# The first FFN half-step computed from an x that is loaded with features on partitions and left unscaled, with the inverse roots applied behind the products

## The chip, the core and the metric

The kernel runs on one core of one Trainium2 chip. The time is device microseconds of one execution; several runs of a kernel agree within about 0.2%. The profile is taken from one execution by the hardware profiler. TensorE is called PE (its weight loads PEld), VectorE DVE, ScalarE ACT, GpSimd POOL; SP only issues DMAs. SBUF has 128 partitions; matmul results go to banks of PSUM, 128 x 512 words of float32 each.

## What is computed

One layer of a decoder block for 1024 tokens of 1024 features in float32. The change lies in the first half-step and touches nothing behind it:

```python
def rms_norm(x, g):
    xf = x.astype(jnp.float32)
    y = xf * lax.rsqrt(jnp.mean(xf * xf, axis=-1, keepdims=True) + RMS_EPS)
    return (y * g.astype(jnp.float32)).astype(x.dtype)

def swiglu(x, w1, w3, w2):
    return (jax.nn.silu(x @ w1) * (x @ w3)) @ w2

h = h + 0.5 * swiglu(rms_norm(h, ffn1_norm[l]), ffn1_w1[l], ffn1_w3[l], ffn1_w2[l])
# then the mixers, h = h + merged @ w_out[l], the second half-step and the last norm
```

`w1` and `w3` are 1024 x 2816, `w2` is 2816 x 1024. The root in `rms_norm` is one number for each token, the gain `g` one for each feature.

## The kernel before, in words

**Seven products.** Each large matrix product is made from 2 x 2 blocks with seven products in place of eight (class `Sevens`, L306). For `x @ w1` the blocks of x are the halves of the tokens and of the features, with features on partitions: b11 and b21 are the low and high features of tokens 0 to 511, b12 and b22 those of tokens 512 to 1023. The seven right operands are b11, b21, b22 and the sums t1 = b12 - b11, t2 = b22 - t1, t3 = b22 - b12 and t4 = t2 - b21. Every operand is held as a high part in a rounded type and a low part, the remainder; ACT makes the high part and DVE or POOL the low one, and a product takes three of the four combinations: twelve matmuls of 128 x 512 (`product`, L325).

**Pairs and quads.** The 22 column blocks of each factor are taken two at a time: 11 pairs (class `Pair`, L565), each with a quad A of `w1` and a quad B of `w3` (class `Quad`, L336). A quad's weight blocks come as two rows, `raw`, of 512 KB. `operand(m)` forms the weight operand m and splits it into four rotating places `wc`; `run(m)` issues the product. Products 1 and 2 of a quad, with b11 and b21, add up in one bank; 3 and 5 in another. `a_out` and `b_out` take a bank's contents: for m = 1 ACT copies it before m = 2 may add to it, for m = 2 of quad A a silu follows. From the opening on there are four banks of each of the two kinds (`mm`, `acc`).

**The opening** (`begin_up1`, L981, an order written out by hand, as are all parts under `manual_schedule`: each engine runs its instructions in the order in which they are written). Rows of x, 128 tokens each, are loaded, squared on ACT, their roots taken on POOL (`inverse`, L277), and multiplied by root and gain on DVE. Then PE transposes them, four 128 x 128 pieces at a time, into a bank (`Rows`, L402; `turned` in `Entry.run`, L483), from which ACT takes the high part and DVE the low part and the sums. While the first rows are on their way, four products of pairs 4 and 5 are made from x loaded with features on partitions (`led_run`); they are scaled later by the roots spread over columns (`means`), stored in DRAM and fetched in pairs 4 and 5. The first two products of pairs 0 to 2 run between the transposes.

**Behind it.** `up` (L692) runs the other five products of pairs 0 to 2 by hand, operands two products ahead of their use, then pairs 3 to 9, whose order the framework sets, then pair 10 by hand. `Down` (L778) multiplies by `w2`, with tokens on partitions, and `add` (L871) adds half of each result to the rows of x.

Loads of x and of weights go through SP's queue in order of writing; the gains and the rows of x for `add` through ACT's.

Of the kernel before, what the change touches and what calls it, by code (L numbers as in the profile page):

```python
# [16 lines left out]
P = 128  # L17
# [120 lines left out]
def tile_block(  # L138
# [145 lines left out]
    def scaled_part(t, c, gain):  # L284
        ve.scalar_tensor_tensor(h[t][:, c], h[t][:, c], inv[t][:, 1:2], gain[:, c], op0=OP.mult, op1=OP.mult)

# [19 lines left out]
    class Sevens:  # L306


        def __init__(self, name, X, fw, fs=None):
            self.name, self.X, self.fw, self.fs = name, X, fw, fs or fw  # L310
            self.n_lo = 0
            self.terms = (0, 1, 2)
            self.led = {}
# [251 lines left out]
    class Pair:  # L565
# [3 lines left out]
        def __init__(self, sv, j, sums, early=False, spare=False):  # L569


            self.sv, self.j, self.sums = sv, j, sums
            self.place_of = [h_tile if spare else tmp, h_tile if early else tmp]
            self.u2 = (lambda n: h_tile(f"u2_{n}")[:, :HALF]) if spare else (lambda n: sv.half_tile("u", n))
            self.y = []
            self.A, self.B = Quad(sv, f"{j}a"), Quad(sv, f"{j}b")
            self.u = {}
            self.led = sv.led.get(j)
            self.order = ORDER if self.led is None else (2, *(m for m in ORDER if m not in (1, 2)))
# [5 lines left out]

        def fetch_a(self):
            if self.led is not None:
                nc.sync.dma_start(self.place(0, slice(HALF, S)), self.led[0])

        def fetch_b(self):  # L590
            if self.led is not None:
                self.u[2] = self.u2(f"{self.j}2")
                nc.sync.dma_start(self.u[2], self.led[1])
# [7 lines left out]
        def a_out(self, m, p):  # L601
# [7 lines left out]
            elif m == 2:  # L609
                c = self.place(0, lows)  # L610
                if self.led is not None:
                    ve.tensor_tensor(c, p, u2, op=OP.add)
                    p = c
# [3 lines left out]
            elif m == 5:  # L617
                c22 = self.place(1, highs)
                ve.tensor_tensor(c22, p, self.place(1, lows), op=OP.add)
                ac.activation(c22, c22, AF.Silu)  # L620
            elif m == 4:
                u3 = self.place(1, lows)
                ve.scalar_tensor_tensor(u3, p, -1.0, u3, op0=OP.mult, op1=OP.add)
                ac.activation(u3, u3, AF.Silu)
            else:
                ve.tensor_tensor(u2, p, u2, op=OP.add)
                ac.activation(u2, u2, AF.Silu)

        def b_out(self, m, p):
# [7 lines left out]
            elif m == 2:  # L637
                c = self.place(0, lows)
                if self.led is not None:
                    u[3] = self.sv.half_tile("u", f"{j}3")  # L640
                    ve.tensor_tensor(u[3], p, u[2], op=OP.add)
                    p = u[3]
                ve.tensor_tensor(c, p, c, op=OP.mult)
            elif m == 7:
                if 3 not in u:
                    u[3] = self.sv.half_tile("u", f"{j}3")
# [45 lines left out]
    def up(sv, sums, between, name, room, begun):  # L692
# [31 lines left out]
        for j in range(len(begun), NPAIR - 1):  # L724
            q, then = then or Pair(sv, j, sums), None
            for m in q.order[:3]:
                q.a(m)
            q.fetch_b()
            for m in q.order[3:]:
                q.a(m)  # L730
            if j == NPAIR - 2:
                between()
            if j + 1 in sv.led:
                then = Pair(sv, j + 1, sums)
                then.fetch_a()
            for m in q.order[:-2]:
                q.b(m)
# [4 lines left out]
            for m in q.order[-2:]:  # L742
                q.b(m)
# [34 lines left out]
    class Down:  # L778
# [3 lines left out]
        def __init__(self, name, sums, half_tile, pair):  # L782
# [7 lines left out]
            self.right, self.apart = {}, set()  # L790
            downs.append(self)
# [139 lines left out]
    for t in range(NT):  # L931
        h.append(h_tile(f"x{t}"))

    def load_rows(*ts):
        for t in ts:
            nc.sync.dma_start(h[t], x[t * P:(t + 1) * P, :])

    gain_row = keep.tile([P, D], F32, tag="gain", bufs=1, name="gain_ffn1")
    led_x, led_in = [], []
    for n in range(2):  # L940
        led_x.append(row(f"led_x{n}").rearrange("p (k c) -> p k c", k=2))
        led_in.append(row(f"led_w{n}").rearrange("p (k c) -> p k c", k=2))
    square = X["t1"][0][:, 0:2, :].rearrange("p k c -> p (k c)")
    square2 = tmp("square2")

    LED = (4, 5)
    led_dram = [dram.tile([P, HALF], F32, name=f"led{q}") for q in range(4)]

    def load_all():
        def features(kk):  # L950
            nc.sync.dma_start(led_x[kk], x_t[0, kk])

        def weight(q):
            nc.sync.dma_start(led_in[q // 2][:, q % 2], (w1a, w3a)[q % 2][2 * LED[q // 2]][:, LOWS])

        features(0)
        weight(0)
        weight(1)
        features(1)
        load_rows(0)  # L960
        weight(2)
        load_rows(1)
        weight(3)
        load_rows(2, 3)
        raws.depth = 2
        raws.load()
        load_rows(4)
        raws.depth = 3
        raws.load()
        load_rows(5)  # L970
        raws.depth = 4
        raws.load()
        load_rows(6, 7)
        raws.depth = 6
        raws.load()
# [5 lines left out]
    def begin_up1():  # L981


        load_all()
        idle = bank("mm", "idle")

        def keep_on(n):

            for _ in range(n):
                pe.matmul(idle[:, :P], ones, ones, start=True, stop=True)  # L990

        def spread(p, columns):
            for k, c in enumerate(columns):
                pe.transpose(p[:, k * P:(k + 1) * P], c.to_broadcast([P, P]), ident)
            return p

        def gains(b):
            return spread(bank("acc", f"gain{b}"), [gain1[:, k:k + 1] for k in range(4 * b, 4 * b + 4)])

        def gain_copy(b):  # L1000
            ac.activation(gain_row[:, (LOWS, HIGHS)[b]], g[b], AF.Copy)

        r = {}

        def rows(t, what, c, tag="acc", eng=ac):
            r[t] = Rows(X, what, h[t][:, c], t, tag, eng=eng)

        def first_scaled(t):
            ve.scalar_tensor_tensor(h[t][:, LOWS], h[t][:, LOWS], inv[t][:, 1:2], g[0], op0=OP.mult, op1=OP.mult)

        xhi, xlo = X["t4"]
        kept = [sv1.half_tile("s", f"led{q}") for q in range(4)]
        means = sv1.half_tile("u", "means")
        led_w, led_p = {}, {}

        def led_high(k, eng=ac):
            if eng is ac:
                ac.activation(xhi[:, k], led_x[k // 2][:, k % 2], AF.Copy, scale=gain1[:, k:k + 1])
            else:
                ve.tensor_scalar(xhi[:, k], led_x[k // 2][:, k % 2], gain1[:, k:k + 1], None, op0=OP.mult)  # L1020

        def led_low(k):
            ve.scalar_tensor_tensor(xlo[:, k], led_x[k // 2][:, k % 2], gain1[:, k:k + 1], xhi[:, k].bitcast(F32),
                                    op0=OP.mult, op1=OP.subtract)

        def led_split(q, c):
            if q not in led_w:
                led_w[q] = fp.tile([P, 2, HALF], F32R, tag="wc", bufs=4, name=f"wc_led{q}")
            w, src = led_w[q], led_in[q // 2][:, q % 2]
            ac.activation(w[:, 0, c], src[:, c], AF.Copy)  # L1030

        def led_rest(q, c):
            w, src = led_w[q], led_in[q // 2][:, q % 2]
            gp.tensor_tensor(w[:, 1, c], src[:, c], w[:, 0, c].bitcast(F32), op=OP.subtract)

        FRONT, BACK, WHOLE = slice(0, 2 * P), slice(2 * P, HALF), slice(0, HALF)
        count = {}

        def led_run(q, ks, terms):
            w = led_w[q]  # L1040
            if q not in led_p:
                led_p[q] = bank("mm", f"u_led{q}")
                count[q] = 0
            for i in terms:
                for k in ks:
                    r = slice(k * P, (k + 1) * P)
                    a, b = three((w[:, 0, r], w[:, 1, r]), (xhi[:, k, :], xlo[:, k, :]))[i]
                    pe.matmul(led_p[q], a, b, start=count[q] == 0, stop=count[q] == 11)
                    count[q] += 1

        def led_scaled(q):
            ve.tensor_tensor(kept[q], kept[q] if q < 2 else led_p[q], means, op=OP.mult)
            nc.sync.dma_start(led_dram[q], kept[q])
            sv1.led.setdefault(LED[q // 2], [None, None])[q % 2] = led_dram[q]

        keep_on(13)
        led_high(0)
        led_high(1, ve)
        led_split(0, FRONT)
        led_split(0, BACK)  # L1060
        led_rest(0, FRONT)
        led_low(0)
        led_low(1)
        led_rest(0, BACK)
        led_split(1, FRONT)
        led_rest(1, FRONT)
        led_split(1, BACK)
        led_rest(1, BACK)
        led_run(0, (0, 1), (0, 1, 2))
        g = {}  # L1070
        for b in (1, 0):
            g[b] = gains(b)
        led_run(1, (0, 1), (0, 1, 2))
        led_high(2)
        led_high(3, ve)
        led_low(2)
        led_low(3)
# [1433 lines left out]
```

## Time and profile before

| what | us |
|---|---|
| median of 3 runs | 1885.16 (1884.06 to 1885.36) |
| the profiled execution | 1884.1 |
| its span | 1882.3 |
| mean granted clock of PE | 0.999 of full speed |
| first matmul of a product | 6.38 from the span's start |
| first matmul of `Down` of the first half-step | 434.3 |

A page of a profile gives each engine's busy time and a strip of 40 slices of the span, one digit for tenths of busy time. Other views list groups of equal instructions, the instructions in order of time (start, duration, name, and in brackets the engine's idle time and what ended it) and busy time in chosen stretches. In names like `u_f10a` the letters behind f1 are pair and quad: pair 0, quad A. Matmuls overlap: one lasts 0.39 us and the next begins 0.23 us after it began.

### The profile page before, as it was taken

The page shows a single profiled execution, that of the slowest core. Times are in us where ns is not written, and L with a number is a line of the kernel's source. Part 1 is how long each engine was busy: PE and PEld are TensorE (multiplying, and loading weights), DVE is VectorE, ACT ScalarE, POOL GpSimd, SP SyncE. Part 2 cuts the span into 40 slices and gives each one's busy share as a digit, 9 for nine tenths or more (in the row PEclk, how much of TensorE's full clock was granted, in tenths as well). Part 3 has the DMA queues.
Part 4 walks back from the last instruction along what each step waited for, and adds up shares of the span by engine and source line. Part 5 has one row for each costly group of instructions (what it writes and reads, how often), then busy time and mean ns, then how long its engine had stood idle before and what let it go on. Part 6 is the DMA issues. An engine that isn't in the chain of part 4 may idle for free.

```text
span 1882.3 us, 24614 instructions
## 1 busy us (share of the span) xinstructions
PE 1872.2 (99%) x8758; PEld 1554.8 (83%) x8758; DVE 1349.0 (72%) x1981; ACT 773.4 (41%) x1395; POOL 727.7 (39%) x543
## 2 busy tenths in 40 slices
PE   9999999999999999999999999999999999999998
PEld 8888888888888888888888888888888888888886
DVE  7877666558786776658885897787765566577867
ACT  7433333334344543334445772363333333334344
POOL 4533333331223364444554457545333333312221
PEclk9999999999999999999999999999999999999999
DMA  6154323336565526765578878634332233354654
GB/s 248 56 201 163 128 100 116 115 118 222 177 224 196 182 91 221 243 219 188 209 254 315 313 227 294 262 147 172 125 139 85 89 107 111 136 200 156 225 197 146
DMA packets 146035, 334.98 MB, mean 178 GB/s; under 512 B 17784, under 2 KB 39288, under 8 KB 144376
## 3 DMA queue, kind: packets, MB, share of 16 engines
q1 hardware_dynamic: 142168, 322.55, 49.7%
q10 hardware_dynamic: 3744, 10.85, 1.6%
q8 instruction: 69, 1.13, 0.2%
q14 instruction: 54, 0.44, 0.1%
HBM read 232.76 MB, written 100.60 MB: 177 GB/s over the span
## 4 chain that ended last, share of the span: by engine, by line
PE 54%; DVE 3%; ACT 2%; issue 1%; DMA 1%; POOL 1%; ACTq 0%; SPq 0%; DVEq 0%; POOLq 0%
PE u_mixm L332 15%; PE d_f L869 8%; PE wo L2191 4%; PE yp L1933 1%; PE u_f20a L332 1%; PE u_f21b L332 1%; PE u_f20b L332 1%; PE u_f21a L332 1%; PE u_f210b L332 1%; PE u_f210a L332 1%; PE u_f29b L332 1%; PE u_f29a L332 1%; PE u_f28b L332 1%; PE u_f28a L332 1%; PE u_f27b L332 1%
## 5 line engine op out<-in xcount | busy, mean ns | idle before, releaser
L869 PE MATMUL d_f<-bhi_f,ahi_f 128*128 128x512 f32 x616 | 240.2, 390 | 0.0
L869 PE MATMUL d_f<-bhi_f,alo_f 128*128 128x512 f32 x616 | 239.7, 389 | 0.0
L869 PE MATMUL d_f<-blo_f,ahi_f 128*128 128x512 f32 x616 | 239.6, 389 | 0.0
L826 POOL TENSOR_TENSOR alo_f<-g_f,ahi_f 128x512 fp32r<-128x512 f32 x60 | 86.0, 1450 | 273.6 <-ACT ahi_f L822 273.6
L332 PE MATMUL u_mixm<-xhi_t_mix,wc_mixm 128*128 128x512 f32 x608 | 157.3, 391 | 0.6 <-ACT wc_mixm L320 0.6
L869 PEld LDWEIGHTS d_f<-bhi_f,ahi_f 128*128 128x128 f32 x616 | 115.7, 188 | 24.1 <-ACT h L422 0.5
L869 PEld LDWEIGHTS d_f<-bhi_f,alo_f 128*128 128x128 f32 x616 | 115.6, 188 | 24.1
L869 PEld LDWEIGHTS d_f<-blo_f,ahi_f 128*128 128x128 f32 x616 | 115.7, 188 | 23.9
L332 PEld LDWEIGHTS u_mixm<-xhi_t_mix,wc_mixm 128*128 128x128 f32 x608 | 113.5, 188 | 24.4 <-ACT wc_mixm L320 1.1
L332 PE MATMUL u_mixm<-xhi_b_mix,wc_mixm 128*128 128x512 f32 x456 | 120.3, 391 | 0.0
L323 POOL TENSOR_TENSOR wc_mixm<-s_mixm,wc_mixm 128x512 fp32r<-128x512 f32 x52 | 77.1, 1483 | 102.1 <-ACT wc_mixm L320 102.1
L332 PEld LDWEIGHTS u_mixm<-xhi_b_mix,wc_mixm 128*128 128x128 f32 x456 | 85.0, 188 | 17.2
L320 ACT ACTIVATE wc_mixm<-s_mixm 128x512 fp32r<-128x512 f32 x76 | 47.0, 628 | 112.2 <-DVE s_mixm L376 57.2
L822 ACT ACTIVATE ahi_f<-g_f 128x1024 fp32r<-128x1024 f32 x84 | 81.9, 975 | 4.1 <-DMA g_f<-gs_f 4.1
L332 PE MATMUL u_mixm<-xlo_t_mix,wc_mixm 128*128 128x512 f32 x304 | 81.3, 389 | 0.0
L323 POOL TENSOR_TENSOR wc_mixm<-raw,wc_mixm 128x512 fp32r<-128x512 f32 x41 | 62.3, 1523 | 37.5 <-ACT wc_mixm L320 31.8
L2191 PE MATMUL wo<-w_o,o_hi 128*128 128x512 f32 x224 | 69.4, 391 | 0.1
L822 ACT ACTIVATE bhi_f<-s_f2w 128x512 fp32r<-128x512 f32 x55 | 32.9, 628 | 86.7 <-DVE s_f2w L844 67.8
L822 ACT ACTIVATE bhi_f<-s_f1w 128x512 fp32r<-128x512 f32 x55 | 33.0, 629 | 83.1 <-DVE s_f1w L844 69.9
L332 PEld LDWEIGHTS u_mixm<-xlo_t_mix,wc_mixm 128*128 128x128 f32 x304 | 57.1, 188 | 12.0
L826 DVE TENSOR_TENSOR alo_f<-g_f,ahi_f 128x1024 fp32r<-128x1024 f32 (+1 forms) x48 | 57.6, 1200 | 8.5 <-ACT ahi_f L822 8.5
L332 PE MATMUL u_mixm<-xlo_b_mix,wc_mixm 128*128 128x512 f32 x228 | 61.0, 389 | 0.0
(1359 smaller groups left out, 4768.1 us busy)
## 6 DMA issues: line engine op xcount, KB each, us to landing
g_f<-gs_f SPq DMA_DIRECT2D x70, 512.0 KB
gs_f<-y_f SPq DMA_DIRECT2D x88, 256.0 KB
raw<-in_w2a_dram SPq DMA_DIRECT2D x35, 512.0 KB
raw<-in_w2b_dram SPq DMA_DIRECT2D x35, 512.0 KB
gs_f<-gb_f SPq DMA_DIRECT2D x46, 256.0 KB
raw<-in_w1a_dram SPq DMA_DIRECT2D x22, 512.0 KB
raw<-in_w3a_dram SPq DMA_DIRECT2D x22, 512.0 KB
raw<-in_w1b_dram SPq DMA_DIRECT2D x22, 512.0 KB
```

What stands on the lines that cost most here:

```text
L320: ac.activation(w[:, 0], src, AF.Copy)
L323: eng.tensor_tensor(w[:, 1], src, w[:, 0].bitcast(F32), op=OP.subtract)
L332: pe.matmul(p, a, b, start=(start and n == 0), stop=(n == 11), skip_group_check=not start)
L822: ac.activation(hi[:, c], src, AF.Copy)
L826: eng.tensor_tensor(lo[:, d], src[:, o], hi[:, d].bitcast(F32), op=OP.subtract)
L869: pe.matmul(self.banks[m][t], l, r, start=(first and q == 0), stop=(last and q == 2))
L1933: pe.matmul(p, a, b, start=(j == 0), stop=(j == 11))
L2191: pe.matmul(banks[m][t], l, r, start=(st == 0 and j == 0 and q == 0), stop=(st == 1 and j == 1 and q == 2))
```

## The change

x is loaded a second time with features on partitions, all of it (eight tiles `x_t`, one for two groups of 128 features and half the tokens). The eight operands are formed from these tiles by DVE, ACT and POOL, with the gain and without the root: steps `step1` to `step3` turn the tiles in place into t1, t2, t3 and t4. No row of x is transposed. The roots, of squares that ACT takes from rows loaded into free places, come in two groups of four (`inverses`), and PE spreads them over columns with eight transposes (`spread`). The first factor's sums are multiplied by them ahead of each silu: by DVE out of the bank for m = 2, by POOL in SBUF for m = 5, 4 and 3 (`lit`). The second factor stays unscaled, and `add` multiplies by half the root of each token, a column, in place of 0.5. The four early products of pairs 4 and 5 are gone; the opening begins with pair 0's own.

```diff
             elif m == 2:
                 c = self.place(0, lows)
+                if self.sv.norm is not None:
+                    ve.tensor_tensor(c, p, self.sv.norm[:, lows], op=OP.mult)
                     p = c
                 ac.activation(c, p, AF.Silu)
...
-                ac.activation(c22, c22, AF.Silu)
+                self.lit(c22, highs)
...
+        def lit(self, c, cols):
+            if self.sv.norm is not None:
+                gp.tensor_tensor(c, c, self.sv.norm[:, cols], op=OP.mult)
+            ac.activation(c, c, AF.Silu)
...
-                ve.scalar_tensor_tensor(hs, self.banks[m][t], 0.5 * sign, hs, op0=OP.mult, op1=OP.add)
+                by = 0.5 * sign
+                if self.halves is not None:
+                    by = self.halves[sign][:, 4 * th + t:4 * th + t + 1]
+                ve.scalar_tensor_tensor(hs, self.banks[m][t], by, hs, op0=OP.mult, op1=OP.add)
...
+        features(0, 0)
+        weight(0, LOWS)
+        weight(1, LOWS)
+        features(0, 1)
+        weight(0, HIGHS)
+        features(0, 2)
+        features(0, 3)
+        weight(1, HIGHS)
+        more(4)
+        row_places()
+        features(1, 0)
+        features(1, 2)
+        load_rows(0, 1, 2, 3)
+        features(1, 1)
+        features(1, 3)
+        more(6)
...
+        def step1(k):
+            ve.tensor_tensor(xt(1, k), xt(1, k), xt(0, k), op=OP.subtract)
+            ve.tensor_scalar(xt(1, k + 4), xt(1, k + 4), gain(k + 4), None, op0=OP.mult)
+
+        def step2(k):
+            low("t1", k, xt(1, k), gain(k))
+            ve.scalar_tensor_tensor(xt(1, k), xt(1, k), less[:, k:k + 1], xt(1, k + 4), op0=OP.mult, op1=OP.add)
+
+        def step3(k):
+            ve.scalar_tensor_tensor(xt(0, k), xt(0, k), less[:, k:k + 1], xt(1, k), op0=OP.mult, op1=OP.add)
+            ve.scalar_tensor_tensor(xt(0, k + 4), xt(0, k + 4), less[:, k + 4:k + 5], xt(1, k),
+                                    op0=OP.mult, op1=OP.add)
+
+        def squares_of_x(t):
+            for n, (r, _) in enumerate(rows_of_x[t % 4]):
+                ac.activation(r, r, AF.Square, accum_out=means[:, n, t:t + 1])
...
+        operand(4, 2)
+        for k in (2, 3):
+            high("t2", k, xt(1, k))
+            low("t2", k, xt(1, k))
+        out(3, 2)
+        for k in range(4):
+            step3(k)
+        squares_of_x(5)
+        squares_of_x(6)
+        run(5, 1)
+
+        out(5, 1)
+        operand(5, 2)
+        squares_of_x(7)
+        squares_of_x(4)
+        inverses(1)
+        run(4, 2)
+        p = spread(1)
+
+        operand(0, 6)
+        spread_copy(1, p)
+        for k in range(4):
+            high("t3", k, xt(0, k))
+            low("t3", k, xt(0, k))
+        out(4, 2)
+        run(5, 2)
+        operand(0, 7)
+        for k in range(4):
+            high("t4", k, xt(0, k + 4))
+            low("t4", k, xt(0, k + 4), eng=gp)
+        out(5, 2)
...
-        gains_of.append(load_gain(mix_norm, "mix"))
...
+        gains_of.append(load_gain(mix_norm, "mix"))
+        down.halves = halves
```

Three places show what stands in the engines' rows now. First DVE in the opening, from the low parts of the first operands on. Before, it takes them from banks (`x_b11` is a bank with a transposed row) beside scaling rows of x:

```order
L1009 SCALAR_TENSOR_TENSOR x1_134<-x1_134,nst_1_307,gain0_269 128x512
L418 TENSOR_TENSOR xlo_b11_f1_124<-x_b11_0_315,xhi_b11_f1_123 128x4x128
L278 TENSOR_SCALAR nst_2_323<-nst_2_323 128x1
L415 CAST xhi_b11_f1_123<-x_b11_1_339 128x4x128
L1009 SCALAR_TENSOR_TENSOR x2_135<-x2_135,nst_2_323,gain0_269 128x512
L278 TENSOR_SCALAR nst_3_325<-nst_3_325 128x1
L418 TENSOR_TENSOR xlo_b11_f1_124<-x_b11_1_339,xhi_b11_f1_123 128x4x128
```

Now it takes them from the tiles in SBUF (`x_t02` holds the third pair of feature groups of the first tokens):

```order
L1002 TENSOR_SCALAR xhi_b11_f1_123<-x_t00_143,gain1_109 128x512
L1009 SCALAR_TENSOR_TENSOR xlo_b11_f1_124<-x_t00_143,gain1_109,xhi_b11_f1_123 128x512 x2
L1002 TENSOR_SCALAR xhi_b11_f1_123<-x_t01_144,gain1_109 128x512
L1009 SCALAR_TENSOR_TENSOR xlo_b11_f1_124<-x_t01_144,gain1_109,xhi_b11_f1_123 128x512 x2
L1002 TENSOR_SCALAR xhi_b21_f1_127<-x_t03_146,gain1_109 128x512
L1009 SCALAR_TENSOR_TENSOR xlo_b21_f1_128<-x_t02_145,gain1_109,xhi_b21_f1_127 128x512 x2
L1009 SCALAR_TENSOR_TENSOR xlo_b21_f1_128<-x_t03_146,gain1_109,xhi_b21_f1_127 128x512 x2
```

The bank as a source is gone: each of these low parts reads two tiles of SBUF.

Second ACT in the later part of the opening. Before, from the first high part of b22 on, one square (`square2`) stands among high parts (`xhi`), splits of weights (`wc`) and a silu (`y`):

```order
L413 ACTIVATE xhi_b22_f1_121<-x_b22_4_542 128x4x128
L614 ACTIVATE y_f10_0_446<-u_f10a1_391 128x512
L435 ACTIVATE xhi_t2_f1_125<-x_t2_4_550 128x4x128
L435 ACTIVATE xhi_t1_f1_131<-x4_137 128x4x128
L320 ACTIVATE wc_f11b2_570<-raw3_216 128x512
L435 ACTIVATE xhi_t3_f1_129<-x_b12_4_537 128x4x128
L274 ACTIVATE square2_146,nst_6_578<-x6_139 128x1024
L320 ACTIVATE wc_f12a1_582<-raw4_220 128x512
```

Now, from the last high parts of t2 to the copy of the second group's spread roots (L1042), where `means` takes the sums of squares (line numbers from here on are those of the changed kernel; its L317 is L320 of before):

```order
L1000 ACTIVATE xhi_t2_f1_125<-x_t11_142 128x512 x2
L1026 ACTIVATE u_f1row1_0_211,means_134<-u_f1row1_0_211 128x512
L1026 ACTIVATE u_f1row1_512_212,means_134<-u_f1row1_512_212 128x512
L1026 ACTIVATE s_f1row2_0_213,means_134<-s_f1row2_0_213 128x512
L1026 ACTIVATE s_f1row2_512_214,means_134<-s_f1row2_512_214 128x512
L625 ACTIVATE u2_last_147<-u_f12b1_508 128x512
L317 ACTIVATE wc_f12b2_522<-raw5_230 128x512
L1026 ACTIVATE s_f1row3_0_215,means_134<-s_f1row3_0_215 128x512
L1026 ACTIVATE s_f1row3_512_216,means_134<-s_f1row3_512_216 128x512
L1026 ACTIVATE row_x_210,means_134<-row_x_210 128x1024
L317 ACTIVATE wc_f10a6_552<-s_f10a2_550 128x512
L1042 ACTIVATE norm_ffn1_148<-norm1_543 128x512
```

The squares of four rows stand together ahead of the spread, three of them in halves, since their places are weight places of half a row each.

Third POOL at the end of the opening, where pair 0's operands are made. Before, a low part of t1 and one of t4 stand among the low parts of weights:

```order
L376 TENSOR_TENSOR s_f10a2_710<-s_f10a1_704,raw0_208 128x512
L323 TENSOR_TENSOR wc_f10a6_740<-s_f10a2_710,wc_f10a6_740 128x512
L323 TENSOR_TENSOR wc_f10a7_760<-s_f10a3_758,wc_f10a7_760 128x512
L438 TENSOR_TENSOR xlo_t1_f1_132<-x7_140,xhi_t1_f1_131 128x4x128
L323 TENSOR_TENSOR wc_f10a5_767<-s_f10a1_704,wc_f10a5_767 128x512
L438 TENSOR_TENSOR xlo_t4_f1_120<-s_f1t4_5_641,xhi_t4_f1_119 128x4x128
L323 TENSOR_TENSOR wc_f10a4_778<-raw6_580,wc_f10a4_778 128x512
```

Now, from the second group's roots (L1032) on, with `lit` in L617:

```order
L1032 TENSOR_TENSOR roots_135<-means_134,fours_133 128x4
L320 TENSOR_TENSOR wc_f10a6_552<-s_f10a2_550,wc_f10a6_552 128x512
L320 TENSOR_TENSOR wc_f10a7_582<-s_f10a3_580,wc_f10a7_582 128x512
L1007 TENSOR_TENSOR xlo_t4_f1_120<-x_t02_145,xhi_t4_f1_119 128x512 x2
L1007 TENSOR_TENSOR xlo_t4_f1_120<-x_t03_146,xhi_t4_f1_119 128x512 x2
L320 TENSOR_TENSOR wc_f10a5_597<-s_f10a1_548,wc_f10a5_597 128x512
L320 TENSOR_TENSOR wc_f10a4_613<-raw6_383,wc_f10a4_613 128x512
L617 TENSOR_TENSOR y_f10_1_648<-y_f10_1_648,norm_ffn1_148 128x512
L320 TENSOR_TENSOR wc_f10b6_657<-s_f10b2_655,wc_f10b6_657 128x512
L320 TENSOR_TENSOR wc_f10b7_675<-s_f10b3_673,wc_f10b7_675 128x512
```

All four low parts of t4 stand ahead of the low part of operand 5 (`wc_f10a5`), and the first multiplication by the roots stands behind that of operand 4.

More of the change, by code (lines that the diff above doesn't have):

```diff
@@ L732, in up @@
                 between()
[L733 to L736, printed above, removed]
+            for m in ORDER[:-2]:
                 q.b(m)
@@ L938, in tile_block @@
[L938 to L947, printed above, removed]
-    def load_all():
[L950 to L975, printed above, removed]
+            for r, c in rows_of_x[t % 4]:
+                nc.sync.dma_start(r, x[t * P:(t + 1) * P, c])
@@ L984, in begin_up1 @@
         load_all()
+        sv1.norm = norm
         idle = bank("mm", "idle")
[L987 to L994, printed above, removed]
-            return p
-        def gains(b):
-            return spread(bank("acc", f"gain{b}"), [gain1[:, k:k + 1] for k in range(4 * b, 4 * b + 4)])
@@ L1037, in begin_up1 @@
[L1037 to L1043, printed above, removed]
+        for _ in range(13):
+            pe.matmul(idle[:, :P], ones, ones, start=True, stop=True)
+        ve.memset(fours, -0.5)
+        ve.memset(means, 0.0)
+        ve.tensor_scalar(less, gain1, -1.0, None, op0=OP.mult)
+        pairs = [Pair(sv1, j, sums, True, (lambda n: u2_last[:, :HALF]) if j == 2 else None) for j in range(3)]
@@ L1107, in begin_up1 @@
[L1107 to L1119 removed]
+                    a, b = three((w[:, 0, r], w[:, 1, r]), (hi[:, k, :], lo[:, k, :]))[i]
@@ L1120, in begin_up1 @@
+        high("b21", 6, xt(0, 6), gain(6))
+        high("b21", 7, xt(0, 7), gain(7), ve)
+        for k in range(4, 8):
+            low("b21", k, xt(0, k), gain(k))
+        out(0, 1)
+        operand(1, 2)
         sv1.terms = (0, 2, 1)
-        entry.product(0)
+        run(0, 2)
+        out(1, 1)
+        operand(2, 1)
+        run(1, 2)
         sv1.terms = (0, 1, 2)
-        ac.activation(means, p, AF.Copy)
-        entry.operand(1)
-        led_scaled(2)
-        for t in (2, 3):
-            r[t].keep(h[t][:, LOWS])
```

333 lines of the change are left out of this document (158 added, 175 removed).

## The prediction, as it was made

> **What bounds the kernel now.** First the page: its share of busy time, and the strip of 40 slices (busy tenths of PE).
>
> ```profile
> span 1882.3 us, 24614 instructions
> PE 1872.2 (99%) x8758; PEld 1554.8 (83%) x8758; DVE 1349.0 (72%) x1981; ACT 773.4 (41%) x1395; POOL 727.7 (39%) x543
> ...
> PE   9999999999999999999999999999999999999998
> ```
>
> PE is never without work in any slice, so time can be won only by taking instructions from PE, and every wait that PE gets is lost in full. Then the timeline of PE (start, us, instruction) at the first product, in the row stage and behind the first factor of pair 0.
>
> ```profile
> 1.05 5.50 PE L990 MATMUL idle<-ones 128*128 128x128 f32 x26 [1.05 <-DVE mhalf L198]
> 6.38 0.73 PE L1048 MATMUL u_led<-xhi_t_f,wc_led 128*128 128x512 f32 x2
> ...
> 46.98 1.07 PE L332 MATMUL u_f12a<-xlo_b_f,wc_f12a 128*128 128x512 f32 x4
> 47.89 1.08 PE L332 MATMUL u_f12a<-xhi_b_f,wc_f12a 128*128 128x512 f32 x4
> 48.80 0.60 PE L487 MATMUL x_b<-ident,x 128*128 128x128 f32 x4
> 49.24 0.60 PE L411 MATMUL x_b<-ident,x 128*128 128x128 f32 x4
> 49.60 1.17 PE L332 MATMUL u_f12b<-xhi_b_f,wc_f12b 128*128 128x512 f32 x4
> 50.61 1.08 PE L332 MATMUL u_f12b<-xlo_b_f,wc_f12b 128*128 128x512 f32 x4
> ...
> 72.55 1.07 PE L332 MATMUL u_f10b<-xhi_t_f,wc_f10b 128*128 128x512 f32 x4
> ```
>
> Four matmuls step by 0.91 us, so a product of twelve takes 2.72. From 48.80 to 50.61 lie eight transposes and four matmuls: 1.81 - 0.91 = 0.90 for the eight, 0.11 each. From 6.38 to 72.55 PE does 21 products (57.2 us) and the transposes; the groups of PE's lines give their count.
>
> ```profile
> L411 PE MATMUL x_b<-ident,x 128*128 128x128 f32 x48 | 6.9, 273 | 0.0
> ...
> L487 PE MATMUL x_b<-ident,x 128*128 128x128 f32 x16 | 2.4, 272 | 0.0
> L994 PE MATMUL gain<-ident,gain 128*128 128x128 f32 x8 | 1.0, 272 | 0.0
> L994 PE MATMUL means<-ident,nst 128*128 128x128 f32 x4 | 0.6, 272 | 0.0
> ```
>
> 76 x 0.1125 = 8.5; 57.2 + 8.5 = 65.7 of 66.2 us. The opening holds half a microsecond of waiting, no more.
>
> **What is removed.** 76 transposes go, 8 come (four roots twice): 68 x 0.1125 = **7.65 us won**, if PE still never waits. The products keep their number: the four early ones of pairs 4 and 5 return as ordinary ones. The copies of the led results through DRAM lie beside PE and are worth nothing.
>
> **What it costs is waiting,** since DVE, ACT and POOL now make the operands from SBUF, in an order with little lead. Prices first. Stretches of the opening and of the pairs behind it (us, then busy of PE, PEld, DVE, ACT, POOL, clock, DMA share, GB/s), and ACT's timeline:
>
> ```profile
> 5.00:10.00 5.00, 5.00 (x30) 4.36 (x29) 3.25 (x5) 3.41 (x8) 3.12 (x4) 1.00 1.00 350
> 10.00:15.00 5.00, 5.00 (x26) 4.11 (x25) 4.10 (x9) 4.75 (x10) 3.63 (x4) 1.00 1.03 415
> 15.00:20.00 5.00, 5.00 (x32) 4.24 (x31) 3.73 (x8) 3.93 (x10) 2.37 (x4) 1.00 1.03 413
> 20.00:25.00 5.00, 5.00 (x28) 4.17 (x27) 4.89 (x7) 3.05 (x8) 1.29 (x1) 1.00 1.02 404
> ...
> 60.00:98.00 38.00, 38.00 (x169) 31.42 (x169) 31.62 (x44) 13.40 (x23) 17.51 (x14) 1.00 0.15 49
> ```
>
> ```profile
> 8.16 0.72 ACT L1018 ACTIVATE xhi_t_f<-led_x,gain 128x512 fp32r<-128x512 f32 x1 [0.81 <-DMA led_x<-in_x_t_dram]
> ...
> 28.66 1.06 ACT L274 ACTIVATE square<-x 128x1024 f32<-128x1024 f32 x1
> ...
> 29.70 0.63 ACT L320 ACTIVATE wc_f11b<-raw 128x512 fp32r<-128x512 f32 x1
> 30.22 0.60 ACT L634 ACTIVATE u_f<-u_f10b 128x512 f32<-128x512 f32 x1
> 30.70 0.64 ACT L320 ACTIVATE wc_f10a<-raw 128x512 fp32r<-128x512 f32 x1
> ```
>
> ACT steps by 0.5 for 128x512 and 1.04 for a row's square. A square of half a row does not occur; it lies between 0.5 and 1.04, and I take 0.62 (half of 1.04 and a second start). At 8.16 the first 1.57 MB are usable (the second feature piece behind one more and two weight halves of 256 KB, the same four loads as in the new order). Behind it the new order's pieces go at 0.37 MB a microsecond while small ones run (350 to 415) and at 0.41 then: the feature pieces of the second operand (0.79 and 1.31 MB on) are there by 10.3 and 11.7, row 0 of x (4.2 MB on) by 18.7, row 3 by 22.5. DVE and POOL, apart and together:
>
> ```profile
> 44.17 0.69 DVE L418 TENSOR_TENSOR xlo_b_f<-x_b,xhi_b_f 128x512 fp32r<-128x512 f32 x1 [0.23 <-ACT xhi_b_f L413]
> 44.78 0.69 DVE L473 TENSOR_TENSOR x_t<-x_b,x 128x512 f32<-128x512 f32 x1
> ...
> 53.21 0.69 DVE L476 TENSOR_TENSOR x_b<-x_t,x 128x512 f32<-128x512 f32 x1
> 53.81 0.68 DVE L438 TENSOR_TENSOR xlo_t_f<-x_t,xhi_t_f 128x512 fp32r<-128x512 f32 x1
> ```
>
> ```profile
> 62.97 1.58 DVE L438 TENSOR_TENSOR xlo_t_f<-x,xhi_t_f 128x512 fp32r<-128x512 f32 x1
> ```
>
> ```profile
> 44.42 0.55 POOL L279 TENSOR_TENSOR nst<-nst,mhalf 128x1 f32<-128x1 f32 x1
> ...
> 53.34 1.29 POOL L438 TENSOR_TENSOR xlo_t_f<-x,xhi_t_f 128x512 fp32r<-128x512 f32 x1 [1.40 <-ACT xhi_t_f L435]
> ```
>
> ```profile
> 62.71 1.29 POOL L438 TENSOR_TENSOR xlo_t_f<-x,xhi_t_f 128x512 fp32r<-128x512 f32 x1
> 63.96 1.74 POOL L323 TENSOR_TENSOR wc_f10a<-s_f10a,wc_f10a 128x512 fp32r<-128x512 f32 x1
> 65.66 1.29 POOL L438 TENSOR_TENSOR xlo_t_f<-s_f1t,xhi_t_f 128x512 fp32r<-128x512 f32 x1
> 66.92 1.75 POOL L323 TENSOR_TENSOR wc_f10a<-raw,wc_f10a 128x512 fp32r<-128x512 f32 x1
> ```
>
> DVE steps by 0.60, POOL by 1.26, a root costs 0.55. At 53.3 a DVE operation with one input in a bank (x_b, x_t) runs beside POOL untouched. At 62.97 one with both inputs in SBUF waits until POOL is through at 63.96 and then takes its 0.6; POOL's next, due at 63.96, waits for it (1.74). So they **take turns, 1.86 us a turn**. Before, most DVE work of the opening reads banks; afterwards nearly all of it reads SBUF twice.
>
> With these prices I follow each engine's order (names: product (n, m) is factor n with operand m; factors 0 and 1 are pair 0's two, and so on).
>
> 1. Operand b21, low parts. PE could end (0,2) at 6.38 + 3 x 2.72 = 14.5. ACT makes two high parts from 10.3, then a split (11.8), a high part, and copies and splits by turns, so POOL can start four weight low parts at 12.0, 13.4, 14.4 and 15.4; DVE has four x low parts from 12.2 (11.7 and its own high part). 12.2 + 4 x 1.86 = 19.65, and the last matmul ends at 20.0: **5.5** late.
> 2. First spread of roots. Four products: PE is ready at 20.0 + 10.9 = 30.9. ACT stands at the copy out of (2,1), at 25.5; behind it a split and two high parts (27.7), four half squares (30.2), a copy and a split (31.2); POOL's low part 32.9, root 33.5: **2.6**.
> 3. Product (4,1) needs the bank of (0,2), which DVE's multiplication by the roots frees. From 33.5 POOL and DVE take turns over three POOL low parts and five DVE steps: 40.9, against 34.0 + 2.72: **4.3**.
> 4. (4,2): its split stands on ACT behind a silu that waits for another such multiplication (46.5): 48.2 against 46.4: **1.9**.
> 5. Second spread. PE is there at 51.0. ACT's squares are done at 55; DVE has eight steps of t3 and t4 and one turn, 51.4 + 4.8 + 1.3 = 57.5, then the root: 58.3: **7.3**.
> 6. Pair 0's operand 7: DVE's four low parts of t3 begin after a POOL low part (60.8), then a multiplication and the operand's own difference (64.4); silu and split 65.2. PE is ready at 58.8 + 2 x 2.72 = 64.2: **1.1**.
> 7. Its operand 5: the low part stands on POOL behind four low parts of t4. From 66.5: 4 x 1.26 + two DVE steps = 72.8, then 1.26 = 74.0; due at 68.0 + 1.8 = 69.8: **4.3**.
>
> Sum 27.0. The second matter is `lit`: 33 POOL multiplications of about 1.29 (nearest row: 65.66). On the chain product, DVE 0.6, a turn, POOL, silu 0.5, next split 0.5, that is up to 5.5 us against two products (5.44). In the opened pairs 0 to 2 and the last pair, where operands are made two products ahead, I take 1 us a pair, 3 in all (pair 0 is in terms 6 and 7); in pairs 3 to 9 a silu stands about four products ahead, and POOL goes from 12-17 to 16-21 of 38 us: nothing. Bounds: 0 and, with each of the nine later ones uncovered by half a turn, 8. On SP the later rows of x and the second halves of pair 0's weights stand behind places that come free late (the rows' by 30.2, term 2; the weights' when POOL is through with b22, near 47); they are wanted at 49 and 57.5, and a load takes some 4 us from its issue, as the first piece does (0.74 to 4.50). Without that cover it would be term 5 that grows.
>
> ```profile
> 0.74 0.38 SPq L951 DMA_DIRECT2D led_x<-in_x_t_dram  x1
> ...
> 4.50 0.72 ACT L1018 ACTIVATE xhi_t_f<-led_x,gain 128x512 fp32r<-128x512 f32 x1 [1.34 <-DMA gain<-in_ffn_norm_dram]
> ```
>
> The additions take a column in place of a constant; L1009, the nearest row, already does (0.745 mean against 0.68), PE covers it, and 48 x 0.06 = 3 would be its price without cover. The later gain load has the whole down stage to land.
>
> ```profile
> L1009 DVE SCALAR_TENSOR_TENSOR x<-x,nst,gain 128x512 f32<-128x512 f32 x4 | 3.0, 745 | 1.0 <-POOL nst L279 0.9
> ```
>
> 27.0 + 3 - 7.65 = **+22.4**. The profiled execution took 1884.1 (1.8 around its span; the median of the runs is 1885.16): **1906.5**.
>
> **Rivals.**
> - *No turns* (both engines read SBUF at will, as at 53.3). The same walk with bare durations leaves 1.3 (the copy out of (0,1), behind the last feature piece, ends at 13.1, PE is free of (1,1) at 11.8), 2.3 (ACT's squares end at 26.0, the root at 29.0, PE is there at 26.8), 0.2 (the bank), 5.1 (squares end at 44.4, root 45.7, PE 40.6), 0.8 and 3.1 (POOL's row of t4 low parts alone) = 12.9: 12.9 - 7.65 = +5.2, **1889**. Against it is 62.97. If DVE keeps the port over several steps while POOL waits (no row shows that), it is about 1901. Together 0.18.
> - *PE slow after a stop.* Terms 3, 5 and 7 are waits of over 4 us. The 26 idle matmuls after PE's first idle microsecond step by 0.21 (5.50 in all) against 0.11 for a transpose of the same shape, which is another operation: bounds 0 and half of 5.5 for each stop, 0 to 8. The forecast takes 0, the rival some 5: **1911**. Against it: the clock column is 1.00 from the start. 0.14. The Trainium skill, TensorE: Matmul & The Clock Gate, Part 1, says that about 3.4 us of idling halve PE's clock until about 3.4 us of work; by that rule each stop loses 1.7, an estimate, and the sum would be 1911.6; no run here shows a stop.
> - *Not slower.* The squares and roots are done in ACT's and DVE's gaps before each spread, and neither port nor bank holds PE: terms 2, 3 and 5 vanish, 1.3 + 0.8 + 3.1 = 5.2 of waiting remains, **1881.7**; with the rest gone too, 1876.5. It decides from where PE's waits sum to under 7.65. For it: before, ACT has a fifth of 10 to 25 free (11.73 of 15 busy). Against it: row 0 is not there before 18.7, and behind it ACT works without a gap to 31. 0.10.
>
> **How the numbers follow.** Forecast 0.58, its own range 1901 to 1910. The range takes in both slow rivals and part of `lit`'s bound: 1889 to 1914, leaving some 0.15. A measurement of this kernel tells 0.2% (3.8 us) from no change: faster 0.05, same 0.05, slower 0.90.
>
> **What would show it.** Right: PE waits at the last low parts of b21 (12 to 20), before both spreads (2 to 3 and 5 to 8 us), at the bank of (4,1), and in pair 0's operand 5 behind t4's low parts; DVE low parts of 1.2 to 1.8 us while POOL works; pair 0's first factor done at about 80.5 (17 products, 46.2, two spreads, 0.9, and 27.0, behind 6.38), where 72.55 closed 21 products; no further loss after pair 2. Wrong: DVE at 0.6 beside POOL, or squares done before PE is at a spread; or an added wait per pair all through to 434, which would make `lit` the main cost.

## The result, and the profile after

1929.8 us (median of 6 runs, 1928.35 to 1930.64) against 1884.74 (1884.06 to 1885.39): ratio 1.0238, 95% interval 1.0225 to 1.0251. The sign was forecast; 1906.5 was too little by 23, and 1914 was not enough for the range. The profiled execution took 1930.07, its span 1928.2. First its page:

```profile
span 1928.2 us, 24498 instructions
## 1 busy us (share of the span) xinstructions
PE 1894.8 (98%) x8690; PEld 1549.5 (80%) x8690; DVE 1369.0 (71%) x1972; ACT 768.8 (40%) x1398; POOL 776.1 (40%) x571
...
PE   8799999999999999999999999999999999999998
```

PE has 68 instructions less, as worked out, and is busy 22.6 us *longer* (1894.8 against 1872.2). Waits don't make an engine busy: something is slower. Then what PE waited for from 6 to 81 us (us in total, times, longest):

```profile
PE norm L1038 <- POOL roots L1032: 11.3, 2, 8.2
PE u_f10a L329 <- POOL wc_f10a L320: 2.8, 1, 2.8
PE u_f12a L329 <- DVE y_f L598: 1.5, 1, 1.5
PE u_first L329 <- DVE xlo_b_f L1009: 1.5, 2, 1.2
PE u_f12a L329 <- ACT wc_f12a L317: 1.2, 1, 1.2
PE u_first L1078 <- ACT wc_first L1064: 0.5, 1, 0.5
PE u_first L329 <- ACT y_f L592: 0.4, 1, 0.4
PE u_first L1078 <- DVE xlo_b_f L1009: 0.2, 1, 0.2
```

19.4 us in sum, 18.3 of them at places that were forecast: the two spreads (`norm`), the low part behind t4's on POOL (`wc_f10a`), the bank (`y_f` L598), the split of (4,2) (`wc_f12a`), b21's low parts (`xlo_b_f` in L329). Then PE's timeline (start, us, instruction) in the opening, behind it and in the steady pairs:

```profile
18.07 3.55 PE L329 MATMUL u_first<-xhi_b_f,wc_f10b 128*128 128x512 f32 x8
...
58.91 1.12 PE L1038 MATMUL norm<-ident,roots 128*128 128x128 f32 x4 [8.19 <-POOL roots L1032]
...
80.80 1.10 PE L329 MATMUL u_f10b<-xhi_t_f,wc_f10b 128*128 128x512 f32 x4
...
300.03 1.10 PE L329 MATMUL u_f16b<-xhi_b_f,wc_f16b 128*128 128x512 f32 x4
300.96 1.10 PE L329 MATMUL u_f16b<-xhi_t_f,wc_f16b 128*128 128x512 f32 x4
301.90 1.10 PE L329 MATMUL u_f16b<-xlo_t_f,wc_f16b 128*128 128x512 f32 x4
```

Pair 0's first factor is done at 80.80; 80.5 was forecast. But look at 300: four matmuls step by 0.933, where 0.907 stood before: 0.2333 us a matmul against 0.2267, in a stretch without a wait, at a granted clock of 1.00. And the eight matmuls from 18.07 on begin 0.43 us apart. What that is, the view by stretches shows (us, PE busy, granted clock, DMA share, GB/s):

```profile
14.60:18.00 3.40, 1.92 (x7) 1.00 1.02 404
18.00:21.40 3.40, 3.40 (x9) 0.50 1.06 390
...
31.60:35.10 3.50, 1.06 (x7) 0.99 0.78 277
35.10:38.50 3.40, 3.40 (x10) 0.50 0.24 49
...
55.50:62.40 6.90, 3.50 (x11) 0.51 0.23 77
```

Three stretches in which PE waited much are followed by half clock: at 18.0, 35.1 and 55.5. From the starts of PE's matmuls these three cost 4.2 us, counted from one matmul of a product to the next, and 4.8 with the transposes and the first matmul behind the last wait.

The slower step is a matter of its own. It reaches where the change has no line: the mixers' products (`u_mixm`, 685 to 1072 us). Groups of before, with mean ns of one behind the busy time:

```profile
L869 PE MATMUL d_f<-bhi_f,ahi_f 128*128 128x512 f32 x616 | 240.2, 390 | 0.0
L332 PE MATMUL u_mixm<-xhi_t_mix,wc_mixm 128*128 128x512 f32 x608 | 157.3, 391 | 0.6 <-ACT wc_mixm L320 0.6
```

and of after:

```profile
L850 PE MATMUL d_f<-bhi_f,ahi_f 128*128 128x512 f32 x616 | 240.2, 390 | 0.0
L329 PE MATMUL u_mixm<-xhi_t_mix,wc_mixm 128*128 128x512 f32 x608 | 161.0, 397 | 0.0
```

`Down` (`d_f`) keeps its 390 ns; the mixers' products go from 391 to 397. So the 45.9 us of span divide like this (first matmuls of pair 0's quad B and of `Down`; before, four more products, 10.9 us, lay ahead of the first mark):

| stretch | before | after | later by |
|---|---|---|---|
| to pair 0's first factor | 72.55, 61.65 without the four | 80.80 | 19.1 |
| from there to `Down` | 361.8, 372.7 with the four | 390.3 | 17.6 |
| `Down` to the end | 1448.0 | 1457.1 | 9.1 |

Of the 17.6, 137 products x 12 x 6.6 ns are 10.9 and the rest, 6.7, are waits with the restarts behind them: PE is idle for 4.2 us between 81 and 480, and the first matmul behind a wait takes longer (1.20 in place of 1.10 for four). Behind the start of `Down` the step alone accounts for the 9.1: the four groups of `u_mixm` hold 1596 matmuls, 10.5 us at 6.6 ns each, and of the runs below e1, with the step of before, takes 1447.6 us there, e2, with the slower step and no line of the change, 1457.4.

### The profile page after: what moved, and what is told of

Read it like the earlier page. It is cut to its first block, busy times and chain, and to the rows that moved or that the text cites. A ratio compares the mean times of both kernels' runs of the same rounds, so it can differ in the third digit from the quotient of the medians.

```text
span 1928.2 us, 24498 instructions
## 1 busy us (share of the span) xinstructions
PE 1894.8 (98%) x8690; PEld 1549.5 (80%) x8690; DVE 1369.0 (71%) x1972; ACT 768.8 (40%) x1398; POOL 776.1 (40%) x571
## 4 chain that ended last, share of the span: by engine, by line
PE 83%; DVE 3%; ACT 2%; POOL 1%; issue 1%; DMA 1%; SPq 0%; ACTq 0%; POOLq 0%; DVEq 0%
PE u_mixm L329 19%; PE d_f L850 18%; PE wo L2216 4%; PE yp L1958 1%; PE u_f18b L329 1%; PE u_f15b L329 1%; PE u_f19a L329 1%; PE u_f18a L329 1%; PE u_f16b L329 1%; PE u_f16a L329 1%; PE u_f15a L329 1%; PE u_f13b L329 1%; PE u_f19b L329 1%; PE u_f20a L329 1%; PE u_f21b L329 1%
## 5 line engine op out<-in xcount | busy, mean ns | idle before, releaser
L329 PE MATMUL u_mixm<-xhi_t_mix,wc_mixm 128*128 128x512 f32 x608 | 161.0, 397 | 0.0
L329 PEld LDWEIGHTS u_mixm<-xhi_t_mix,wc_mixm 128*128 128x128 f32 x608 | 113.6, 188 | 27.2 <-ACT wc_mixm L317 0.2
L850 PEld LDWEIGHTS d_f<-bhi_f,alo_f 128*128 128x128 f32 x616 | 115.6, 188 | 24.5 <-DVE alo_f L807 0.2
L329 PE MATMUL u_mixm<-xhi_b_mix,wc_mixm 128*128 128x512 f32 x456 | 123.0, 397 | 0.0
L320 POOL TENSOR_TENSOR wc_mixm<-s_mixm,wc_mixm 128x512 fp32r<-128x512 f32 x52 | 78.4, 1508 | 105.9 <-ACT wc_mixm L317 83.8
L329 PEld LDWEIGHTS u_mixm<-xhi_b_mix,wc_mixm 128*128 128x128 f32 x456 | 85.0, 188 | 19.9
L317 ACT ACTIVATE wc_mixm<-s_mixm 128x512 fp32r<-128x512 f32 x76 | 47.0, 628 | 107.8 <-DVE s_mixm L373 63.0
L329 PE MATMUL u_mixm<-xlo_t_mix,wc_mixm 128*128 128x512 f32 x304 | 83.2, 395 | 0.0
L618 ACT ACTIVATE y_f<-y_f 128x512 f32<-128x512 f32 x66 | 41.7, 632 | 99.0 <-POOL y_f L617 84.4
L320 POOL TENSOR_TENSOR wc_mixm<-raw,wc_mixm 128x512 fp32r<-128x512 f32 x41 | 60.7, 1484 | 41.9 <-ACT wc_mixm L317 37.4
L329 PEld LDWEIGHTS u_mixm<-xlo_t_mix,wc_mixm 128*128 128x128 f32 x304 | 57.1, 188 | 13.8
```

The costliest lines, as they stand in the source:

```text
L317: ac.activation(w[:, 0], src, AF.Copy)
L320: eng.tensor_tensor(w[:, 1], src, w[:, 0].bitcast(F32), op=OP.subtract)
L329: pe.matmul(p, a, b, start=(start and n == 0), stop=(n == 11), skip_group_check=not start)
L618: ac.activation(c, c, AF.Silu)
L850: pe.matmul(self.banks[m][t], l, r, start=(first and q == 0), stop=(last and q == 2))
```

## The experiments

**The step: where the operands lie.** The change adds six small tiles to the pool `consts` (224 bytes a partition), and all that is allocated on the left side of SBUF behind that pool moves up: the x operands `xhi` and `xlo` of the first half-step and of the mixers. Their weight operands `wc` are on the right side and stay. `Down` and the second half-step have both operands on the left, and their distance stays. The pool of before even holds two tiles that nobody reads, which set the place of what comes behind:

```python
consts.tile([P, 24], F32, name="pad")
...
consts.tile([P, 32], F32, name="pad2")
```

Five runs add bytes that nobody reads and do nothing else: what is allocated behind them on the same side moves, the operands among it. Changed kernel, x operands (e1):

```diff
+    consts.tile([P, 8], F32, name="pad3")
```

> The changed kernel with one tile of 32 bytes a partition more among the constants, so that the x operands on the left side of SBUF stand 256 bytes behind where they stood before the change instead of 224; nothing else moves. Theory A (the matmul step depends on how the addresses of the x operand and of the weight operand stand to each other, 0.2267 us where they agree and 0.2333 where they are 32 bytes apart): the step is 0.2267 in all stages, some 3200 matmuls x 6.6 ns = 21 us go, 1929.8 falls to about 1909, while PE's waits of the opening (about 20 us) stay. Theory B (the slower step is an after-effect of PE's stops or of the added work on POOL): the step stays 0.2333, the time 1930.

Changed kernel, weight operands (e9):

```diff
+    keep.tile([P, 8], F32, tag="pad_right", bufs=1, name="pad_right")
```

> The changed kernel, order and all, with 32 bytes a partition reserved on the right side of SBUF, so that the weight operands of the first half-step and of the mixers move down by 32 bytes and the x operands stay where the change put them. Theory (the distance between the two operands' addresses decides the matmul step): distance 0 again, a step of 0.2267, about 1913 as in e1. Rival (the place of the x operands alone decides): a step of 0.2333 in these stages and 1930 as the changed kernel.

Kernel before, with 32, 64 and 128 bytes (`[P, 8]`, `[P, 16]`, `[P, 32]`):

> The kernel before with 32 bytes more among the constants, and nothing of the change. Theory A: the step in the pairs of the first half-step and in the mixers' products becomes 0.2333, about 21 to 23 us are lost, 1884.7 becomes 1906 to 1908, with PE still without waits. Theory B: 1884.7 and 0.2267.

> The kernel before with 64 bytes more. Theory A with a period of 64 bytes: 1884.7 and a step of 0.2267. If the period is 128 bytes or more, or any shift from the place found costs something: above 1890.

> The kernel before with 128 bytes more among the constants. If the matmul step depends on the distance of the two operands' addresses modulo 128 bytes: 1884 and a step of 0.2267, as without. If the period is 256 bytes or longer: a step between 0.2267 and 0.2293 and up to 8 us more, as at 64 bytes.

Measured, with the addresses that the program gives to the operands (bytes modulo 512):

| kernel | x operand | weights | distance | `u_mixm`, mean ns | us (median) |
|---|---|---|---|---|---|
| before | 224 | 480 | 256 | 391 | 1884.74 |
| changed | 448 | 480 | 32 | 397 | 1929.80 |
| e1 | 480 | 480 | 0 | 391 | 1912.88 |
| e9 | 448 | 448 | 0 | 391 | 1914.22 |
| e2 | 256 | 480 | 224 | 396 | 1905.85 |
| e3 | 288 | 480 | 192 | 393 | 1891.85 |
| e6 | 352 | 480 | 128 | 396 | 1904.45 |

32 bytes that nobody reads cost the kernel of before 21.8 us (1905.85 against 1884.03 of the same chip; ratio 1.0115, interval 1.010 to 1.013). Moving either operand back gives the old step; in e1 the group reads

```profile
L330 PE MATMUL u_mixm<-xhi_t_mix,wc_mixm 128*128 128x512 f32 x608 | 157.3, 391 | 0.5 <-ACT wc_mixm L318 0.5
```

So it is the distance and not the place of x (e9 against its rival), and no after-effect of waits or of POOL's work (e2 has neither). `d_f`, whose two operands move together, keeps its 390 ns in all seven kernels. The Trainium skill, SBUF — State Buffer, Who interferes with whom, gives PE two SBUF read ports, one for the moving operand and one for weight loads, and calls them independent; by that no distance should matter, and these runs show that one does. Periods of 64 and 128 bytes are out: 64 bytes cost 7.8 us, and 128 cost 20 (a step of 0.2325), where the two cases written down for e6 were nothing and up to 8. Distances 0 and 256 are free, 32 and 224 cost 6 to 7 ns a matmul; the law between is open, and so is what in the chip makes it.

e1 gained 17 where 21 was expected, since it gave part back: with faster products the later waits have less cover. `Down` begins at 463.0 there, so from pair 0's first factor (79.33) it is 383.7 against 372.7: 11 us of waits and restarts instead of 6.7.

**Those later waits: `lit` on DVE** (e5, on top of e1).

```diff
         def lit(self, c, cols):
             if self.sv.norm is not None:
-                gp.tensor_tensor(c, c, self.sv.norm[:, cols], op=OP.mult)
+                ve.tensor_tensor(c, c, self.sv.norm[:, cols], op=OP.mult)
             ac.activation(c, c, AF.Silu)
```

ACT in e1, pair 1, quad B:

```profile
110.41 0.63 ACT L619 ACTIVATE y_f<-y_f 128x512 f32<-128x512 f32 x1 [3.34 <-POOL y_f L618]
110.95 0.62 ACT L318 ACTIVATE wc_f11b<-s_f11b 128x512 fp32r<-128x512 f32 x1
114.21 0.63 ACT L619 ACTIVATE y_f<-y_f 128x512 f32<-128x512 f32 x1 [2.65 <-POOL y_f L618]
114.75 0.61 ACT L318 ACTIVATE wc_f11b<-raw 128x512 fp32r<-128x512 f32 x1
```

ACT stands 3.34 and 2.65 us ahead of silus that wait for POOL, and a split stands behind each; PE, which needs the second split, goes on at 115.41, when that is done.

> As e1 (32 bytes more, the changed kernel's order), with the multiplication by the roots ahead of the silus of m = 5, 4 and 3 on DVE in place of POOL. Theory (behind the opening PE waits because ACT stands at a silu that waits for POOL's multiplication, and the next split or copy stands behind it on ACT): the waits of e1 between 81 and 480 us, 10.7 us in all, fall to under 3, 1912.9 becomes about 1905. Rival (the added multiplication is one operation too many for these engines wherever it stands; DVE, the busier one, is late instead): the time stays within 3 us of 1913.

1902.32 (ratio 1.0092, interval 1.0078 to 1.0106), 10.6 us less than e1. What PE waited for between 81 and 480 us is now one row:

```profile
PE u_f13a L330 <- DVE y_f L606: 0.5, 1, 0.5
```

DVE took the work, 0.6 us in place of POOL's 1.26, and PE waits for nothing else of it.

**The opening's waits: order** (e4, on top of e1). The lines that moved, cut:

```diff
+        squares_of_x(2)
+        squares_of_x(3)
+        load_rows(5, 6, 7, 4)
         out(2, 1)
...
-            low("t4", k, xt(0, k + 4), eng=gp)
+            low("t4", k, xt(0, k + 4))
```

(and `spread(0)`, `spread(1)`, `inverses`, `out(0, 2)` and the other four squares earlier).

> As e1, with the order of the opening changed in these places: squares of rows 2 and 3 ahead of the copy out of (2,1), squares of rows 5, 6, 7 and 4 behind the first multiplications by the roots, both spreads of roots one product behind the roots' end, the multiplications that free the banks of (0,2) and (1,2) ahead of the second half of t1, and the low parts of t4 on DVE in place of POOL. Theory (terms 2 to 5 and 7 are waits for squares, roots and POOL's order, and can be lifted by order alone): against e1 the waits of 3.1, 1.5, 1.2, 8.2 and 2.8 us go and two or three stretches of half clock (about 3 us): some 18 us, so 1891. Rival (the engines' work and not its order holds PE: DVE and POOL by turns): the waits come back at the next operands, and the time stays above 1900.

1911.86 against e1's 1912.88: almost nothing. The time is the one that the rival had; its reason, that no order helps, is not shown by this. What PE waited for from 6 to 81 us:

```profile
PE u_f12b L330 <- ACT wc_f12b L318: 6.8, 2, 4.3
PE u_f12a L330 <- DVE y_f L599: 2.2, 1, 2.2
PE u_f10a L330 <- ACT wc_f10a L318: 2.1, 1, 2.1
PE u_first L330 <- DVE xlo_b_f L1010: 1.5, 2, 1.2
PE norm L1039 <- POOL roots L1033: 1.3, 1, 1.3
```

The waits for roots (11.5 in e1) are down to 1.3, and in their place PE waits for splits: one now stands on ACT behind seven squares, one behind the copy out of (5,1), which waits because its place is that of t2's source, still read by `step3`. The half clock cost more than in e1 (5.4 us against 1.3, from one matmul of a product to the next). A wait moved to the next operand in ACT's row; it was not gone.

So the whole opening was put in another order (e7, and e8 with other choices of engine): each operation where its source is there and no sooner than something wanted earlier on its engine; low parts of weights mostly on DVE. Of e8's text:

```diff
+        operand(1, 2, ve)
+        out(0, 1)
+        operand(2, 1)
...
+        spread_copy(0, p)
+        high("t2", 3, xt(1, 3))
+        root_low(0)
+        high("b22", 7, xt(1, 7))
...
+        high("t3", 0, xt(0, 0))
+        low("t3", 0, xt(0, 0))
+        high("b22", 5, xt(1, 5))
+        silu_low(0)
+        run(2, 2)
```

`root_low` and `silu_low` are the two halves of `out(n, 2)` of a first factor: other work of ACT now stands between them.

> As e5, with the whole opening behind the first two products in another order: squares ahead of copies that are not yet wanted, silus of the first products behind the high parts and splits that the next products need, t3 and t4 formed as soon as their sources are there, most low parts of weights on DVE, low parts of b22 and one of t4 on POOL in its gaps, spreads where their roots are done. Theory (PE's waits of the opening are a matter of order): 5 to 8 us of waits remain to the first factor of pair 0 in place of 22, no half clock behind 30 us; with e5's gain 1884 to 1889. Rival (DVE and POOL reading SBUF by turns cannot make the operands in time in any order): over 12 us of waits remain and the time is over 1895.

> A second order of the same kind, with more low parts of weights on POOL and the low parts of b21 earlier. Same theories: 1884 to 1890 against over 1895.

e7 took 1885.86 (ratio 1.0007, interval 0.9998 to 1.0016), e8 1884.86 (1.0002, 0.9993 to 1.0011): the time of before. e8's waits from 6 to 480 us, all of them:

```profile
PE u_first L330 <- ACT u_f L626: 1.3, 1, 1.3
PE u_f12b L330 <- DVE y_f L1110: 1.2, 1, 1.2
PE u_first L330 <- ACT xhi_b_f L1001: 1.0, 1, 1.0
PE norm L1026 <- POOL roots L1020: 0.9, 2, 0.6
PE u_first L330 <- DVE xlo_b_f L1010: 0.8, 1, 0.8
PE u_f13a L330 <- DVE y_f L606: 0.8, 1, 0.8
PE u_first L330 <- ACT y_f L593: 0.5, 1, 0.5
```

6.5 us, and there is no half clock in it. Pair 0's first factor is done at

```profile
61.93 1.08 PE L330 MATMUL u_f10b<-xhi_t_f,wc_f10b 128*128 128x512 f32 x4
```

and 61.65 was before's time without the four products. Up to there PE is idle for 5.5 us, and the restarts behind its waits take some 2.4: the transposes' 7.65 us are really won, and the waits that were left cost as much. So the rival of e7 and e8 is out: DVE and POOL can make the operands nearly in time. What the order did and what the move of low parts to DVE did was not run apart.

One more try put the first product of pair 1 between pair 0's first two (e10):

> As e8, with the first product of pair 1 ahead of the second products of pair 0 (its weights' first half is loaded ahead of the features of b21), and the order of the rest fitted to that. Theory (what is left of e8's waits, 5 us between 6 and 20 us and 3 behind, lies in the second product of pair 0, which waits for the copy out of its bank and for the low parts of b21; one product between gives both 2.7 us more): 3 us less, 1882. Rival (the loads set the pace there, and the product between only moves the wait): 1885 as e8.

1886.59 (1.0013, 1.0004 to 1.0021): the rival's case, the waits moved, to a bank that pair 2 needs (2.3 us) and to the first spread (1.4). No version was faster than the kernel before.

## Why the prediction was wrong

- **What bounds the kernel, and the 7.65 us of transposes:** right. In e8, 61.93 less its 7.9 us of waits and restarts is 54.0, and 61.65 less 7.65 is the same 54.0.
- **The price of a product, 2.72, was carried through the change:** this step failed. "The products keep their number" is true, but each of 154 products of the first half-step and the mixers' matmuls cost 3% more, 21.8 us by e2. Nothing in the prediction asked what the new tiles in `consts` push aside; no rival had it. The unread `pad` tiles were the sign, and the diff shows allocations, not addresses. That is nearly all of the 23 us. With the operands' distance given back and nothing else (e1) the kernel takes 1912.9, 6.4 above the forecast and inside its range; what is left there is `lit`, below.
- **Terms 1 to 7, 27.0 us:** 19.4 by the view, 4.8 of half clock, 1.4 of the slower step (17 products) and some 1.2 that remain, for the restarts: 26.8 (19.1 + 7.65). That the sum is right is luck: the waits were forecast too long, and what the forecast took at nothing, half clock and step, filled the gap. (Redone from the printed figures, terms 3, 4, 6 and 7 are 0.1 smaller each and the sum of *No turns* is 12.8; nothing hangs on it.) Term 2 (2.6 forecast, 3.1 measured) was right in mechanism. Term 5 (7.3, 8.2) was right in size, but DVE's steps of t3 and t4, forecast as the last, were done when they waited for ACT's squares:

```profile
53.49 0.60 ACT L625 ACTIVATE u_last<-u_f12b 128x512 f32<-128x512 f32 x1 [2.40 <-DVE x_t L1021]
56.90 0.28 DVE L1030 TENSOR_TENSOR means<-means 128x4 f32<-128x4 f32 x1 [0.87 <-ACT row_x L1026]
57.52 1.33 POOL L1032 TENSOR_TENSOR roots<-means,fours 128x4 f32<-128x4 f32 x1 [0.37 <-DVE means L1031]
```

ACT had stood 2.4 us at the copy out of (5,1), whose place `step3` still read, with three squares behind it; and the roots of four rows took 1.33 us, where 0.55 was the price, from one row's. Term 1 (5.5 against 1.9 of waits; PE goes on at 18.07 where 20.0 was forecast), 3 (4.3, 1.5), 4 (1.9, 1.2), 6 (1.1, none) and 7 (4.3, 2.8) were too large. For term 1 the rows of DVE and POOL show why:

```profile
11.83 5.81 DVE L1009 SCALAR_TENSOR_TENSOR xlo_b_f<-x_t,gain,xhi_b_f 128x512 fp32r<-128x512 f32 x4
```

```profile
12.05 1.67 POOL L320 TENSOR_TENSOR wc_f10a<-raw,wc_f10a 128x512 fp32r<-128x512 f32 x1 [2.53 <-ACT wc_f10a L317]
13.67 1.74 POOL L320 TENSOR_TENSOR wc_f10b<-raw,wc_f10b 128x512 fp32r<-128x512 f32 x1
15.38 1.71 POOL L320 TENSOR_TENSOR wc_f11a<-raw,wc_f11a 128x512 fp32r<-128x512 f32 x1
```

- DVE and POOL do take turns, but a turn is 1.7 and not 1.86, and DVE got in first: three turns in place of four. The rival *No turns* is out.
- **PE slow after a stop, taken at 0:** the rival (0.14) was right in kind, 4.8 us where it had 5. The Trainium skill's rule (TensorE: Matmul & The Clock Gate, Part 1) names half clock, and the rows show 0.50; but its condition of about 3.4 us of idling is narrower than the trace: the stretch ahead of 18.0 had PE busy 1.92 of 3.4 us, in waits of 1.2 us at most.
- **`lit`, 3 us and nothing in pairs 3 to 9:** the chain was right, its cover was not. At full step it cost 10.6 us (e5), beyond the bound of 8; with the slow step 6.7, if all of those waits are its own. Of the 4.1 us of idle PE that the view names behind 81, 2.0 lie in pairs 2 and 10, where 3 were forecast with pair 1, and 2.1 in pairs 3 to 8, where the lead of four products was to cover all: 1.1 at a bank, 1.0 at copies out of banks (`u_f`) that stand on ACT behind a silu. "No further loss after pair 2" was wrong.
- **The additions' column, the later gain load, the row loads:** hidden, as said: no row of the waits names them.

Put together: 27.0 + 3 - 7.65 was to be +22.4; 26.8 + 6.7 + 10.9 + 9.1 - 7.65 is 45.9, and without the step's 21.4 (1.4 + 10.9 + 9.1) it is 24.5.

## What to carry to other kernels

Compare the mean duration of an instruction that the change doesn't touch: if it moved, look for what the change moved in memory, and give the operands back their distance, by a pad, before judging the rest. Where one engine takes work in order, price a new wait by what stands behind it, and try the multiplication or copy on another engine first: that alone was worth 10.6 us here. With the operands' distance given back, the same operations take from 1884.9 to 1912.9 us, by their order and by the engine that does `lit` and the low parts.

## What the runs showed of the hardware that was not expected

- The step of a 128x512 matmul depends on the distance of the addresses of its moving operand and its weights: 0.2267 us at 0 and 256 bytes (modulo 512), 0.2333 at 32 and 224, 0.2325 at 128, about 0.229 at 192.
- The half clock goes by windows. In every trace the granted clock keeps each value for 3.41 us or a whole multiple of it, the two ends aside; half clock lasted 3.4, 6.9 or, in e1, 10.2 us. Divide the twelve traces into windows of that length, in step with the clock's changes: each of the 23 at full clock in which PE was busy for at most 1.4 us was followed by half clock, and of all those with 1.5 us and more only one was, the 1.92 us ahead of 18.0. That is why stops of the same place need not bring it: in e1 PE was busy for 1.81 and 1.75 us in the two windows from 27.7 on, and the clock stayed at 1.00. Why the one window differs is open.
